# Where the stored weight sums of two down-projection products are kept, and the order of the last product's token tiles

## The chip, the cores and the metric

The kernel runs on one core of a Trainium2 chip. The metric is the device time of one execution in microseconds. It is written for five engines that run side by side: TensorE (PE, matmuls and transposes), VectorE (DVE), ScalarE (ACT), GpSimd (POOL) and SyncE (SP), which here issues most of the transfers between the memory of the chip and the on-chip buffers.

## The reference

Two layers over 512 tokens of width 1024, in fp32. Each layer mixes tokens and then applies a gated feed-forward part, and each half ends in a layer norm over the sum with its input:

```
for l in range(2):
    mix = token_mixing(x, ...)                      # projections, conv, two attentions, w_o
    x = layer_norm(ALPHA * x + mix, ...)
    h = causal_dwconv(x @ w_up, conv_w) + conv_b    # x: 512 x 1024, w_up: 1024 x 5632
    a, u = split(h)
    x = layer_norm(ALPHA * x + (gelu(a) * u) @ w_down, ...)   # w_down: 2816 x 1024
```

The change is in the last product, `(gelu(a) * u) @ w_down`, the down projection.

## The kernel before, in words

Every fp32 operand of a matmul is split into a high and a low part (`fp32r`), so that one product is three matmuls: high by high, high by low, low by high. For weights, SP loads a slice of up to 128 x 1024 numbers into a buffer `raw`, ACT rounds it into `wh`, and VectorE writes the remainder into `wl` (`unit` and `loaded`). `raw`, `wh` and `wl` rotate over three buffers each, so a slice can be loaded only when a slice three places earlier has been used.

The program is recorded first: every instruction goes to a list, with what it reads and writes (all instructions have line L445 for that reason). `schedule` (L322) then sets the order on each engine. It plays the program with modelled costs and takes, for an engine that is free, the instruction that stands first in the program among those whose inputs and buffers are there. A new place of an instruction in the program, or a new buffer for it, can therefore move others; once set, the order on each engine is fixed, SP's transfers included.

The down projection (`g_down`) saves products: both sides are cut into two by two blocks, and seven products of blocks and of sums of blocks replace eight. In the order of the program they are x1 (weight block 0), x2 (block 2), x6 (weight sum R), x5 (weight sum P), x7 (weight sum Q), x3 (block 3), x4 (weight sum Z); the text calls a product by its left operand or by its weight sum. Each of the seven has six weight slices `u` (the last of half size) and two token tiles of 128 tokens, `i` = 0 and 1, and is 66 matmuls of 128 x 512. `product` runs over the slices, and within a slice over both tiles (`part`); the last two slices are taken together, so that tile 0 is finished a little ahead of tile 1 and `done(0)` (additions to the residual and statistics on VectorE) can begin.

The four weight sums are worked out earlier in the layer and stored in the chip's memory. P and Q are stored whole (`sums`) and are split after loading. R and Z are stored already split (`parts`): `split_before` loads the high part straight into a `wh` buffer and the low part straight into a `wl` buffer, two transfers on SP's queue for a slice.

Three other kinds of buffers matter. `big()` gives one of eleven buffers of 128 x 2048 numbers, which hold the gated inputs of the down projection (`src.h`) and, two slices at a time, the split left operands that `halves` makes. `new_x()` gives the one pair `xh`, `xl` of 128 x 4096 numbers that holds the split input X of a layer's half; it is read for the last time by the last matmul of `w_up`, and taken again when the first tile of the next layer's input is normalized. Matmuls add up in banks: `a` (two of kind `sc`) serve x1, R, Q and Z.

A finished tile of the down projection is normalized by `g_norm`: statistics, a power of -0.5 on GpSimd, two steps on VectorE for each half of the row, a transfer to memory, and in layer 0 eight transposes and a split, which give the next layer's input. Tiles 0 and 1 are finished by x3, tiles 2 and 3 by Z. In the next layer `g_halves` runs its first three projections over tokens 0 to 255 (tiles 0 and 1) and then over tokens 256 to 511, which need tiles 2 and 3; the low parts of their weights are written on GpSimd.

Of the kernel before, what the change touches and what calls it, by code (L numbers as in the profile page):

```python
# [10 lines left out]
F32 = mybir.dt.float32  # L11
F32R = mybir.dt.float32r
# [491 lines left out]
def trunk(ctx, tc, xT_d, x_d, w_d, cst_d, sm_d, w1_d, gb_d, out_d, order):  # L504
# [3 lines left out]
    T, Y = Engine(rec, "PE", nc.tensor), Engine(rec, "SP", nc.sync)  # L508
# [5 lines left out]
    def pool(name, **kw):  # L514
        return ctx.enter_context(tc.tile_pool(name=name, **kw))

    cp = pool("cst", bufs=1)
    sb = pool("sb", bufs=1)
# [12 lines left out]
    cp, sb, smp, ps, dp = (RPool(p) for p in (cp, sb, smp, ps, dp))  # L531

    def nm(s):
        uid[0] += 1
        return f"{s}_{uid[0]}"

    def big(dt=F32):
        return sb.tile([128, 4, 512], dt, tag="big", bufs=11, name=nm("big"))
# [10 lines left out]
    def bank(tag):  # L549
        return ps.tile([128, 512], F32, tag=tag, bufs=dict(mm=3, sc=2, tp=2, pv=1)[tag], name=nm(tag))  # L550
# [14 lines left out]
    def mm3(o, ah, al, bh, bl, start, stop, **kw):  # L565
        mm(o, ah, bh, start, False, **kw)
        mm(o, ah, bl, False, False, **kw)
        mm(o, al, bh, False, stop, **kw)
# [13 lines left out]
    def loaded(src, n, lo=None):  # L582
        raw = sb.tile([128, 1024], F32, tag="raw", bufs=3, name=nm("raw"))
        wh = sb.tile([128, 1024], F32R, tag="wh", bufs=3, name=nm("wh"))
        wl = sb.tile([128, 1024], F32R, tag="wl", bufs=3, name=nm("wl"))
        Y.dma_start(raw[:, :n], src)
        A.activation(wh[:, :n], raw[:, :n], AF.Copy)
        (lo or V).tensor_tensor(wl[:, :n], raw[:, :n], wh[:, :n], op=sub)
        return wh, wl

    def split_before(hi, lo, n):
        wh = sb.tile([128, 1024], F32R, tag="wh", bufs=3, name=nm("wh"))
        wl = sb.tile([128, 1024], F32R, tag="wl", bufs=3, name=nm("wl"))
        Y.dma_start(wh[:, :n].bitcast(F32), hi)
        Y.dma_start(wl[:, :n].bitcast(F32), lo)
        return wh, wl

    def unit(*key, parts=1, lo=None):
        i = len(order)
        order.append(key)  # L600
        n = 1024
        if key[1] == "n_v":
            n = 280 * (key[2][1] - key[2][0])
        if key[1] == "w_dn" and key[3] == NFF // 4:
            n = 512
        raw = sb.tile([128, 1024], F32, tag="raw", bufs=3, name=nm("raw"))
        wh = sb.tile([128, 1024], F32R, tag="wh", bufs=3, name=nm("wh"))
        wl = sb.tile([128, 1024], F32R, tag="wl", bufs=3, name=nm("wl"))
        for p in range(parts):
            c = slice(p * n // parts, (p + 1) * n // parts)  # L610
            Y.dma_start(raw[:, c], w_d[i, :, c])
            A.activation(wh[:, c], raw[:, c], AF.Copy)
            (lo or V).tensor_tensor(wl[:, c], raw[:, c], wh[:, c], op=sub)
        return wh, wl
# [75 lines left out]
    def new_x():  # L690
        return (sb.tile([128, 8, 512], F32R, tag="xh", bufs=1, name=nm("xh")),
                sb.tile([128, 8, 512], F32R, tag="xl", bufs=1, name=nm("xl")))


    def g_down(l, src, r, st, nx, g_norm, last):
# [5 lines left out]
        NM = len(hv)  # L701
        nks = [2] * (NM - 1) + [1]
# [32 lines left out]
        def product(x, w, o, start, done):  # L735

            nu = NM
            kw = {} if start else dict(skip_group_check=True)
            for u in range(nu):
                n = 512 * nks[u]  # L740
                if isinstance(w, int):
                    ws = unit(l, "w_dn", w, u)
                elif w[0] < 2:
                    ws = loaded(src.sums[:, w[0], u * 1024:u * 1024 + n], n)
                else:
                    ws = split_before(*(src.parts[:, 2 * w[0] - 4 + j, u * 1024:u * 1024 + n] for j in range(2)), n)
                if u < nu - 2:
                    group = [(u, ws)]
                    for i in range(2):
                        part(x, group, o[i], i, start and u == 0, False, kw)  # L750
                    yield None
                elif u == nu - 2:
                    group = [(u, ws)]
                else:
                    group.append((u, ws))
                    for i in range(2):
                        part(x, group, o[i], i, False, True, kw)
                        done(i)
                        yield None

        def part(x, group, o, i, start, stop, kw):
            ks = [(u, k, ws) for u, ws in group for k in range(nks[u])]
            for a, (u, k, ws) in enumerate(ks):
                xh, xl = x[2 * u + k]
                c = slice(k * 512, k * 512 + 512)
                mm3(o, xh[:, TOK[i]], xl[:, TOK[i]], ws[0][:, c], ws[1][:, c], start and a == 0, stop and a == len(ks) - 1, **kw)
# [24 lines left out]
        P, Q, R, Z = ([i] for i in range(4))  # L791
        a, b = [bank("sc"), bank("sc")], [bank("pv"), bank("mm")]
        x1 = halves(A(0, 0))
        yield from product(x1, 0, a, True, first_of(0, 0, a, add))
        x2 = halves(A(0, 1))
        yield from product(x2, 2, b, True, then_stats(0, 0, more_of(0, 0, b, add)))
        x6 = halves(A(1, 0))
        yield from product(x6, R, a, False, first_of(0, 1, a, sub))
        c = [bank("mm"), bank("mm")]
        x5 = halves(sums(A(1, 0), A(0, 0)))  # L800
# [8 lines left out]
    def g_tok_norm(l, kind, nk, lhs, res_d, gi, last):  # L809
# [51 lines left out]
        if kind == "w_dn":  # L861
            yield from g_down(l, lhs, r, st, nx, g_norm, last)
            return nx[0], evs, res
# [574 lines left out]
```

## Time and profile before

| what | us |
| --- | --- |
| time, median of 3 runs | 1812.81 |
| lowest and highest of them | 1810.87 and 1815.93 |
| profiled execution | 1815.82 |
| its span | 1813.8 |
| TensorE busy | 1772.5 |
| VectorE, ScalarE, GpSimd busy | 1248.8, 824.9, 227.4 |

The profiled execution is one more execution, with a record of every instruction; its span goes from the first instruction to the last. In the rows below, a line gives when a group of instructions began, how long it was busy, its engine, what it wrote from what (names without their numbers), how many there were, and in square brackets how long the engine had stood still before and what it waited for. TensorE's matmuls overlap, so a single one shows a longer time than the distance to the next: 66 in 14.96 us are 0.227 us each.

### The profile page before, as it was taken

The numbers are of one execution on the slowest core, as the hardware profiler recorded it, in microseconds if no ns is written. First come the engines' busy times: TensorE is split into PE (matmuls) and PEld (weight loads), VectorE is DVE, ScalarE is ACT, GpSimd is POOL, SyncE is SP. The second block draws the span as 40 slices with busy tenths as digits, with TensorE's granted clock in tenths as the row PEclk, the third lists the DMA queues.
The fourth block names the chain that finished last, engine by engine and source line by source line (L and its number), as shares of the span: only waits on it lengthen the run. The fifth ranks groups of instructions, "written<-read, shape, count | busy, mean of one in ns | idle before, by whom it ended". The sixth has DMA issues, their size and how long they took to land.

```text
span 1813.8 us, 23525 instructions
## 1 busy us (share of the span) xinstructions
PE 1772.5 (98%) x8596; PEld 1482.3 (82%) x8596; DVE 1248.8 (69%) x2206; ACT 824.9 (45%) x1418; POOL 227.4 (13%) x302
## 2 busy tenths in 40 slices
PE   8999999999999999999999999999999999999996
PEld 7888888888888888887788887888888888888784
DVE  6978877534458788586679698774344678875884
ACT  4558855322324444354244587553223244444450
POOL 1300023000032110000123001220000411000002
PEclk9999999999999999999999999999999999999998
DMA  6520243233237886446644202332333377763654
GB/s 221 146 98 24 63 131 104 82 107 133 94 104 245 296 293 247 142 156 230 235 157 138 70 34 81 108 105 93 104 129 104 120 274 275 280 235 133 212 195 174
DMA packets 85683, 279.90 MB, mean 154 GB/s; under 512 B 10112, under 2 KB 12256, under 8 KB 85440
## 3 DMA queue, kind: packets, MB, share of 16 engines
q1 hardware_dynamic: 65536, 218.92, 35.4%
q0 software_dynamic: 20032, 59.48, 10.3%
q8 instruction: 68, 1.11, 0.2%
q14 instruction: 47, 0.39, 0.1%
HBM read 223.83 MB, written 42.99 MB: 147 GB/s over the span
## 4 chain that ended last, share of the span: by engine, by line
PE 90%; DVE 3%; DMA 2%; issue 2%; POOL 2%; ACT 1%; SPq 0%; DVEq 0%; POOLq 0%; ACTq 0%
PE mm L445 71%; PE sc L445 11%; PE pv L445 5%; PE tp L445 3%; DVE tmp L445 2%; DMA wh<-parts 1%; POOL wl L445 1%; POOL s L445 1%; DMA raw<-in_w_dram 0%; DMA wl<-parts 0%; DVE st L445 0%; DVE wl L445 0%; DVE s L445 0%; POOL tmp L445 0%; ACT L445 0%
## 5 line engine op out<-in xcount | busy, mean ns | idle before, releaser
L445 PE MATMUL mm<-xh,wh 128*128 128x512 f32 (+1 forms) x1632 | 621.4, 382 | 9.1 <-ACT wh L445 6.1
L445 PE MATMUL mm<-xh,wl 128*128 128x512 f32 (+1 forms) x1632 | 619.0, 380 | 0.6 <-POOL wl L445 0.6
L445 PE MATMUL mm<-xl,wh 128*128 128x512 f32 (+1 forms) x1632 | 619.4, 380 | 0.2 <-DVE xl L445 0.2
L445 ACT ACTIVATE wh<-raw 128x1024 fp32r<-128x1024 f32 (+2 forms) x307 | 317.8, 1038 | 534.5 <-PE mm L445 431.0
L445 DVE TENSOR_TENSOR wl<-raw,wh 128x1024 fp32r<-128x1024 f32 (+3 forms) x292 | 350.7, 1204 | 301.8 <-ACT wh L445 296.6
L445 PEld LDWEIGHTS mm<-xh,wh 128*128 128x128 f32 x1632 | 308.7, 189 | 62.3 <-ACT wh L445 6.5
L445 PEld LDWEIGHTS mm<-xh,wl 128*128 128x128 f32 x1632 | 309.1, 189 | 56.8 <-POOL wl L445 0.8
L445 PEld LDWEIGHTS mm<-xl,wh 128*128 128x128 f32 x1632 | 309.4, 190 | 53.5 <-DVE xl L445 0.8
L445 ACT ACTIVATE tmp<-tmp,s 128x512 f32<-128x512 f32 (+3 forms) x261 | 140.3, 558 | 72.3 <-DVE s L445 39.4
L445 PE MATMUL sc<-wh,big 128*128 128x512 f32 x416 | 136.1, 400 | 11.0 <-DMA wh<-parts 11.0
L445 DVE SCALAR_TENSOR_TENSOR tmp<-mm,smf,tmp 128x511 f32<-128x511 f32 (+1 forms) x176 | 131.1, 745 | 12.7 <-ACT tmp L445 10.5
L445 PE MATMUL mm<-wh,big 128*128 128x512 f32 x380 | 121.7, 390 | 0.0
L445 PE MATMUL mm<-big,wh 128*128 128x512 f32 x384 | 120.0, 391 | 0.0
L445 PEld LDWEIGHTS sc<-wh,big 128*128 128x128 f32 x416 | 80.1, 193 | 31.3 <-DMA wh<-parts 14.6
L445 DVE CUSTOM_DVE_ANT_0 tmp<-sc,cst 128x512 f32<-128x512 f32 (+3 forms) x192 | 89.8, 483 | 21.9 <-PE sc L445 20.5
L445 PE MATMUL tp<-cst,tmp 128*128 128x128 f32 x544 | 86.0, 274 | 5.6 <-DVE tmp L445 2.9
L445 POOL TENSOR_TENSOR tmp<-tmp,cst 128x512 f32<-128x512 f32 (+1 forms) x46 | 48.1, 1053 | 305.2 <-ACT pt L445 119.6
L445 DVE TENSOR_TENSOR big<-big,big 128x512 f32<-128x512 f32 (+3 forms) x114 | 85.8, 767 | 0.4 <-ACT big L445 0.2
L445 PEld LDWEIGHTS tp<-cst,tmp 128*128 128x128 f32 x544 | 67.2, 141 | 21.6 <-DVE xl L445 3.6
L445 ACT ACTIVATE tmp<-tmp 128x512 f32<-128x512 f32 (+2 forms) x68 | 41.1, 605 | 96.0 <-DVE tmp L445 95.8
L445 ACT ACTIVATE big<-big 128x512 fp32r<-128x512 f32 (+2 forms) x86 | 59.2, 713 | 53.9 <-DVE big L445 46.5
L445 PEld LDWEIGHTS mm<-big,wh 128*128 128x128 f32 x384 | 71.7, 188 | 14.4
(149 smaller groups left out, 2243.2 us busy)
## 6 DMA issues: line engine op xcount, KB each, us to landing
raw<-in_w_dram SPq DMA_DIRECT2D x269, 512.0 KB, 3.3
big<-in_w_dram SPq DMA_DIRECT2D x44, 512.0 KB, 5.5
parts<-big POOLq DMA_DIRECT2D x22, 1024.0 KB, 5.6
sums<-big POOLq DMA_DIRECT2D x22, 512.0 KB, 4.4
raw<-sums SPq DMA_DIRECT2D x20, 512.0 KB, 3.6
wl<-parts SPq DMA_DIRECT2D x20, 512.0 KB, 4.9
wh<-parts SPq DMA_DIRECT2D x20, 512.0 KB, 5.8
big<-big POOLq DMA_DIRECT2D x48, 128.0 KB, 2.7
```

Source lines behind the costliest of these rows:

```text
L445: op.call(*[f(x) for x in op.args], **{k: f(v) for k, v in op.kw.items()})
```

## The change

Two of the seven products get their stored sums in other buffers, and one of them another order of its tiles.

- R (x6): the first four slices go into the pair of `new_x()`, high parts into one and low parts into the other, by eight transfers. The last two slices still use `wh` and `wl`.
- Z (x4): all six slices are loaded whole, two slices in a pair of `big` buffers, twelve transfers into six buffers. Then all slices are run for token tile 0, `done(0)` follows, and all slices for tile 1.
- `split_before` is gone; `fetch` issues the two transfers of a slice and `stored` fills a pair of large buffers.

```diff
-    def split_before(hi, lo, n):
-        wh = sb.tile([128, 1024], F32R, tag="wh", bufs=3, name=nm("wh"))
-        wl = sb.tile([128, 1024], F32R, tag="wl", bufs=3, name=nm("wl"))
-        Y.dma_start(wh[:, :n].bitcast(F32), hi)
-        Y.dma_start(wl[:, :n].bitcast(F32), lo)
-        return wh, wl
...
+            if w == Z:
+
+                ws = [stored(w, m, big(F32R), big(F32R)) for m in range((NM + 1) // 2)]
+                for i in range(2):
+                    for u in range(nu):
+                        part(x, [(u, [f[:, u % 2 * 1024:] for f in ws[u // 2]])], o[i], i, False, u == nu - 1, kw)
+                        if u < nu - 1:
+                            yield None
+                    done(i)
+                    yield None
+                return
+            if w == R:
+                early = new_x()
             for u in range(nu):
...
+                elif u < 4:
+                    ws = [f[:, 2 * u:2 * u + 2].rearrange("p a c -> p (a c)") for f in early]
+                    fetch(w, u, ws, n)
                 else:
-                    ws = split_before(*(src.parts[:, 2 * w[0] - 4 + j, u * 1024:u * 1024 + n] for j in range(2)), n)
+                    ws = [sb.tile([128, 1024], F32R, tag=tag, bufs=3, name=nm(tag)) for tag in ("wh", "wl")]
+                    fetch(w, u, ws, n)
...
+        def fetch(w, u, to, n):
+            for j in range(2):
+                Y.dma_start(to[j][:, :n].bitcast(F32), src.parts[:, 2 * w[0] - 4 + j, u * 1024:u * 1024 + n])
+
+        def stored(w, m, *to):
+            to = [f.rearrange("p a c -> p (a c)") for f in to]
+            for u in range(2 * m, min(2 * m + 2, NM)):
+                c = u % 2 * 1024
+                fetch(w, u, [f[:, c:c + 1024] for f in to], 512 * nks[u])
+            return to
```

The order moves at these places. SP's queue in layer 0, at the end of `w_up` and during x1, before (`raw` from `in_w_dram` are slices of weight blocks: `raw_6838` is x1's fifth, `raw_6870` its last, of half size, `raw_6898` x2's first):

```order
L445 DMA raw_6762<-in_w_dram 128x1024
L445 DMA raw_6838<-in_w_dram 128x1024
L445 DMA raw_6870<-in_w_dram 128x512
L445 DMA raw_6898<-in_w_dram 128x1024
L445 DMA raw_6918<-in_w_dram 128x1024
L445 DMA raw_6939<-in_w_dram 128x1024
L445 DMA raw_6974<-in_w_dram 128x1024
```

R's first transfer stands nine places behind x2's first slice there. And after (`raw_6842` is x1's fifth slice, `raw_6880` its last, `raw_6910` x2's first; `xh_6847` and `xl_6834` are the pair of `new_x()`, `parts_5309` the stored sums):

```order
L445 DMA raw_6762<-in_w_dram 128x1024
L445 DMA xl_6834<-parts_5309 128x1024
L445 DMA raw_6842<-in_w_dram 128x1024
L445 DMA xh_6847<-parts_5309 128x1024 x2
L445 DMA xl_6834<-parts_5309 128x1024
L445 DMA xh_6847<-parts_5309 128x1024
L445 DMA xl_6834<-parts_5309 128x1024
L445 DMA raw_6880<-in_w_dram 128x512
L445 DMA xh_6847<-parts_5309 128x1024
L445 DMA xl_6834<-parts_5309 128x1024
L445 DMA raw_6910<-in_w_dram 128x1024
L445 DMA raw_6936<-in_w_dram 128x1024
```

Six of R's eight transfers stand ahead of x1's last slice now, and all eight ahead of x2's first.

TensorE in layer 0 at x1's last slice, before (`sc_6851` is a bank of x1, `pv_6982` and `mm_6995` those of x2):

```order
L445 MATMUL sc_6851<-wh_6891,big_6799 128x512
L445 MATMUL sc_6851<-wh_6921,big_6799 128x512
L445 MATMUL sc_6851<-wl_6931,big_6799 128x512
L445 MATMUL sc_6851<-wh_6921,big_6799 128x512
L445 MATMUL pv_6982<-wh_6956,big_6815 128x512
L445 MATMUL pv_6982<-wl_6965,big_6815 128x512
L445 MATMUL pv_6982<-wh_6956,big_6815 128x512 x2
L445 MATMUL pv_6982<-wl_6965,big_6815 128x512
L445 MATMUL pv_6982<-wh_6956,big_6815 128x512
L445 MATMUL mm_6995<-wh_6956,big_6815 128x512
```

Here x2 follows x1. And after (`sc_6838` and `sc_6855` are x1's banks, and R's too):

```order
L445 MATMUL sc_6838<-wl_6979,big_6799 128x512
L445 MATMUL sc_6838<-wh_6977,big_6799 128x512
L445 MATMUL sc_6855<-wl_6979,big_6799 128x512
L445 MATMUL sc_6855<-wh_6977,big_6799 128x512
L445 MATMUL sc_6838<-xh_6847,big_6955 128x512
L445 MATMUL sc_6838<-xl_6834,big_6955 128x512
L445 MATMUL sc_6838<-xh_6847,big_6955 128x512 x2
L445 MATMUL sc_6838<-xl_6834,big_6955 128x512
L445 MATMUL sc_6838<-xh_6847,big_6955 128x512
L445 MATMUL sc_6855<-xh_6847,big_6955 128x512
```

R's matmuls follow x1's at once; x2's come between later ones of R.

SP's queue in layer 0 ahead of Z, before (`raw_7524` is x3's last slice, `raw_7537`, `raw_7565` and `raw_7570` the next layer's first, `res` the residual that the norm stores):

```order
L445 DMA raw_7524<-in_w_dram 128x512
L445 DMA raw_7537<-in_w_dram 128x1024
L445 DMA raw_7565<-in_w_dram 128x1024
L445 DMA raw_7570<-in_w_dram 128x1024
L445 DMA wl_7575<-parts_5309 128x1024
L445 DMA wh_7580<-parts_5309 128x1024
L445 DMA wl_7596<-parts_5309 128x1024
L445 DMA wh_7603<-parts_5309 128x1024
L445 DMA wh_7612<-parts_5309 128x1024
L445 DMA wl_7614<-parts_5309 128x1024
L445 DMA res_7619<-tmp_6847 128x512
L445 DMA res_7619<-tmp_6859 128x512
```

The next layer's first slices stand ahead of Z's there, and Z's transfers go on, slice by slice, for eight more places between the stores. And after (`big_7525` to `big_7571` are Z's six buffers, `raw_7581` and on the next layer's first slices):

```order
L445 DMA raw_7518<-in_w_dram 128x512
L445 DMA big_7525<-parts_5309 128x1024 x2
L445 DMA big_7533<-parts_5309 128x1024 x2
L445 DMA big_7544<-parts_5309 128x1024
L445 DMA big_7549<-parts_5309 128x1024
L445 DMA big_7544<-parts_5309 128x1024
L445 DMA big_7549<-parts_5309 128x1024
L445 DMA big_7564<-parts_5309 128x1024
L445 DMA big_7571<-parts_5309 128x1024
L445 DMA big_7564<-parts_5309 128x512
L445 DMA big_7571<-parts_5309 128x512
L445 DMA raw_7581<-in_w_dram 128x1024
```

All of Z's transfers stand in a block behind x3's last slice now, and the next layer's first three slices behind them.

## Rows read from the trace of the kernel before

**Rows 1.** The page's busy times of the engines (share of the span, instructions).

```profile
PE 1772.5 (98%) x8596; PEld 1482.3 (82%) x8596; DVE 1248.8 (69%) x2206; ACT 824.9 (45%) x1418; POOL 227.4 (13%) x302
```

**Rows 2.** TensorE's waits: line, what it waited for, us in total, times, longest.

```profile
PE sc L445 <- DMA wh<-parts: 11.0, 9, 2.6
```

**Rows 3.** The chain of waits, layer 0, x1 to R: start, duration (us), work.

```profile
786.26 14.96 PE sc L445 x66
...
812.28 6.42 DMA wh<-parts
...
834.95 5.21 PE mm L445 x23
```

**Rows 4.** The chain of waits, layer 1, x1 to R.

```profile
1684.53 14.96 PE sc L445 x66
...
1713.94 5.85 DMA wh<-parts
...
1732.36 14.96 PE mm L445 x66
```

**Rows 5.** TensorE's timeline, layer 1, Z: start, duration, operation, count, idle before.

```profile
1776.85 0.39 PE L445 MATMUL mm<-wh,big 128*128 128x512 f32 x1
...
1794.10 1.22 PE L445 MATMUL sc<-wh,big 128*128 128x512 f32 x2 [2.44 <-DMA wh<-parts]
...
1801.34 0.39 PE L445 MATMUL sc<-wh,big 128*128 128x512 f32 x1
```

**Rows 6.** Windows: length, busy per engine, clock share (PEclk), transfer share, GB/s.

```profile
884.00:888.00 4.00, 4.00 (x15) 3.19 (x14) 3.83 (x8) 0.25 (x1) 0.78 (x2) 0.77 0.95 310
...
916.00:920.00 4.00, 3.92 (x19) 3.49 (x18) 1.30 (x2) 0.76 (x2) 0.00 (x0) 0.57 0.02 4
...
1796.00:1800.00 4.00, 4.00 (x11) 3.17 (x10) 0.00 (x0) 0.00 (x0) 0.00 (x0) 0.50 0.01 5
818.00:822.00 4.00, 3.26 (x14) 2.71 (x15) 2.09 (x4) 0.00 (x0) 0.00 (x0) 1.00 1.03 414
```

**Rows 7.** TensorE's timeline, layer 0, Z and the passage to layer 1.

```profile
879.44 0.39 PE L445 MATMUL mm<-wh,big 128*128 128x512 f32 x1
881.84 1.78 PE L445 MATMUL tp<-cst,tmp 128*128 128x128 f32 x8 [2.01 <-DVE tmp L445]
...
902.64 0.39 PE L445 MATMUL sc<-wh,big 128*128 128x512 f32 x1
...
914.87 1.26 PE L445 MATMUL tp<-cst,tmp 128*128 128x128 f32 x8 [1.65 <-DVE xl L445]
916.21 0.73 PE L445 MATMUL mm<-xh,wh 128*128 128x256 f32 x3
```

**Rows 8.** The page's transfer issues: count, KB each, us to landing.

```profile
raw<-in_w_dram SPq DMA_DIRECT2D x269, 512.0 KB, 3.3
```

**Rows 9.** VectorE's timeline, layer 0, end of x1.

```profile
795.25 0.68 DVE L445 TENSOR_TENSOR wl<-raw,wh 128x512 fp32r<-128x512 f32 x1
```

**Rows 10.** VectorE's timeline, x4's splits in layers 0 and 1.

```profile
870.11 2.23 DVE L445 TENSOR_TENSOR big<-big,big 128x512 fp32r<-128x512 f32 x4
...
1767.53 2.22 DVE L445 TENSOR_TENSOR big<-big,big 128x512 fp32r<-128x512 f32 x4
```

**Rows 11.** VectorE's timeline, layer 0, normalization of tiles 2 and 3.

```profile
904.79 2.36 DVE L445 SCALAR_TENSOR_TENSOR tmp<-tmp,s,pt 128x512 f32<-128x512 f32 x2
909.96 1.41 DVE L445 SCALAR_TENSOR_TENSOR tmp<-tmp,s,pt 128x512 f32<-128x512 f32 x2 [2.81 <-POOL s L445]
```

**Rows 12.** GpSimd's timeline beside it.

```profile
903.53 2.41 POOL L445 TENSOR_TENSOR wl<-raw,wh 128x1024 fp32r<-128x1024 f32 x1 [2.68 <-ACT wh L445]
```

**Rows 13.** VectorE's timeline, end of the program.

```profile
1801.07 1.38 DVE L445 SCALAR_TENSOR_TENSOR tmp<-tmp,sc 128x512 f32<-128x512 f32 x2 [18.29 <-PE sc L445]
...
1803.99 5.74 DVE L445 SCALAR_TENSOR_TENSOR tmp<-tmp,s,pt 128x512 f32<-128x512 f32 x7
```

**Rows 14.** SP's queue, end of the program.

```profile
1806.76 3.83 SPq L445 DMA_DIRECT2D out_dram<-tmp  x4
```

## The prediction

> **What bounds the kernel now.** I read the page's busy times first: TensorE is busy for 1772.5 us, 98% of the span [rows 1]. So only what TensorE loses can be won, 1813.8 - 1772.5 = 41.3 us of waiting and what a lowered clock adds to the busy time, and each loss has to be found by its place. The list of TensorE's waits came next: the largest item is matmuls into `sc` banks waiting for a transfer of stored weight sums (`wh<-parts`), 11.0 us in 9 waits [rows 2]. The two products that use them are R, the third of the seven products of the down projection, and Z, the last. Then I followed the chain of waits through R. In layer 0 the stretch of x1, x2 and R starts at 786.26 and the next product starts at 834.95 [rows 3]. Each product is 66 matmuls and takes 14.96 us without a gap (the x66 pieces), so three should end at 786.26 + 44.88 = 831.14: R loses 3.8 us. In layer 1 it is 1684.53 + 44.88 = 1729.41 against 1732.36 [rows 4], 2.95 us. In both the chain names the load of `wh` just before the loss: R's slices share three rotating buffers with x2's, so their loads are issued late, and one behind another takes 5.85 to 6.42 us.
>
> For Z I read the timeline of TensorE. In layer 1 x3's last matmul starts at 1776.85 and, at 0.227 us each (14.96 / 66), ends at 1777.08; Z's last starts at 1801.34, so Z takes 24.5 us where 14.96 are needed: 9.5 us lost [rows 5]. The largest wait is 2.44 us, and its price is more than itself: after it the granted clock is 0.50 in the window 1796 to 1800, the lower of the two levels (1.2 and 2.4 GHz) [rows 6]. In layer 0 Z's stretch holds the passage into the next layer too: x3 ends at 879.67, the first transpose waits 2.01 us for DVE (881.84), and after the halves of the next layer's first projections the transposes wait 1.65 us again, so that the second halves start at 916.21 [rows 7], at a clock of 0.57 up to 920 [rows 6], which costs 0.43 x 4 = 1.7 us: as if they had started at 917.9.
>
> **R's loads.** The change issues eight loads of 512 KB as soon as the last `w_up` matmul has read X, at about 786.3 in layer 0, between x1's own weights. A load of 512 KB alone takes 3.3 us [rows 8]; in a full window the queue moves 414 GB/s [rows 6], 1.27 us for each, so 2.03 us of the 3.3 are fixed. Eight loads, x1's fifth and last slices (512 and 256 KB) between them: R's last lands at about 786.3 + 2.0 + 9.5 x 1.27 = 800.4, before x1 ends at 801.22. R's matmuls then run without waits, which gives back 3.8 and 2.95 us.
> What it costs: x1's last slice comes behind six of these loads and lands at about 797.9 instead of some 3 us before its rounding; DVE wrote its low part at 795.25 so far, for 0.68 us [rows 9]. Behind its rounding on ACT (about as long) and DVE's other work of those microseconds it is ready at about 800.9, where TensorE wants it at 801.22 - 6 x 0.227 = 799.9 to 800.2: 0.9 us. R also accumulates into the banks that x1 has just filled, and DVE must read them first: 0.55 us (DVE's 0.68 us less what the other bank covers). Its bounds: 0, if DVE keeps its old order, and 4 us, if x2's first slice, which now also comes behind the burst, is waited for as well. I take 1.45 us a layer, nearer to the first end because x2's matmuls are not wanted until R's have begun. R's part: 3.8 + 2.95 - 2 x 1.45 = 3.85 us.
>
> By the Trainium skill ("DMA: Bandwidth & Descriptors", section "Where 436 GB/s comes from") transfers from HBM to SBUF are held to about 358 GB/s a core, so an estimate is 1.46 us for each load, and R's last would land at 802.2, after x1's end. The window above shows 414 GB/s over four microseconds, and so I keep 1.27; the sum by the rule would be up to 9.5 x 0.19 = 1.8 us a layer less.
>
> **Z's loads.** Twelve loads (ten of 512, two of 256 KB) go into six large buffers that hold until then the split gated inputs (released by x4's splits on DVE, the last of which end at 872.3 and 1769.8 [rows 10]) and x3's first input, released by TensorE two slices into x3, about 870. They start at about 869.2 and 1766.5 and land from 872.5 to 885.3, and from 1770 to 1782.6, 11 x 1.27 + 2 us. TensorE starts Z at 879.7 and 1777.1 and in the new order (tile 0 through all slices, then tile 1) wants slice 2 at 3.2 us (2 x 6 matmuls, and the transposes) and slice 4 at 7.8 us after the start; they land 4.0 and 3.5 us ahead of that. So no wait is left in Z of layer 1: 9.5 us. Its bounds: 0, if the loads wait for the buffers until x3 ends, and 10.3, the clock's share in the last slice included. The cover is a margin of 3.5 us; I take 9.5.
>
> **The tile order.** With tile 0 done half a product (7.5 us) before tile 1, only one tile's normalization stands behind the last matmul. At the end of the program DVE runs seven normalizing steps in 5.74 us, 0.82 each, and two additions and two stats steps [rows 13]; the output's last four transfers start at 1806.76 [rows 14]. From Z's end at 1801.57 to the span's end, 1813.8, are 12.2 us. Three steps (2.46), an addition (0.69) and a stats step (about as long) fewer are 3.8; about 0.8 of it comes back because the one tile must wait for its own power step on GpSimd, which two tiles hid behind each other. I take 3.0, of bounds 1.5 and 3.8.
>
> In the passage between the layers, TensorE must do Z (14.96), 32 transposes (0.16 each at most, by the eight at 914.87) and 72 matmuls of half the columns (0.114 each, 8.2 us) after 879.67: it reaches the second halves at 907.8 if nothing waits. They need tile 3's normalization. In the trace Z's last matmul ends at 902.9 and the second halves start at 916.21 [rows 7], 13.3 us for the normalizations of tiles 2 and 3. With tile 2 done during Z, an addition and a stats step (1.4), four normalizing steps (2.8) and the splits of one tile (about 0.6) go from behind Z, and 8.5 us are left. Z itself now ends at about 897 (14.96 and the transposes of two tiles). That is 905.5, before TensorE wants it. But GpSimd's three splits of the next layer's weights fall into these normalizations: beside one of them (903.53, 2.41 us [rows 12]) two DVE steps took 2.36 us instead of 1.41 [rows 11], and the power step of a normalization queues behind them on GpSimd. One such step late by one or two splits is 907.9 to 910.3, with DVE's own 0.95 us up to 911.3; so the second halves start at about 910 at full clock, against 917.9: I take 8.0, of bounds 4 (a third split ahead of it, and the clock lowered once more) and 10.1, nothing late.
>
> The Trainium skill ("SBUF — State Buffer", section "Who interferes with whom") says why: DVE and GpSimd share a pair of ports, and a DVE instruction with two SBUF inputs blocks against a GpSimd one that reads SBUF. The trace agrees with 0.95 us for two steps. Without this loss the passage would give about 9.
>
> **The sum.** 3.85 + 9.5 + 3.0 + 8.0 = 24.4 us. The profiled execution took 1815.82 us (span 1813.8), so 1791.4 on that; it is 3.0 us above the median of 1812.81, on which it gives 1788.4. I forecast 1789 us.
>
> **The rivals.** *R's burst delays x1 and x2.* If the loads move at the 310 GB/s of the window 884 to 888, whose transfer engines were 95% busy [rows 6], instead of 414, each takes 1.69 us, x1's last slice comes at about 801, x2's first at 806, and three or four microseconds are lost a layer, as much as R wins. For it: TensorE has nothing else to do there, and loads behind others took up to 6.42 us [rows 3]. Against: in the full window of R itself the queue held 414 GB/s. Then R's part is -1 to -4 instead of +3.85: 1793 to 1796.
> *Z's loads come late.* If the first large buffer is released only at x3's end, the first slice lands 2.0 + 2 x 1.27 = 4.6 us after that, and in layer 0 the next layer's first weights stand behind all twelve loads on the in-order queue. Z gains 4 instead of 9.5, the passage 2 instead of 8: 3.85 + 4 + 3 + 2 = 12.9 us in all, 1800, and up to 1804 if those weights are waited for too. Against it stand x4's splits ending 7.4 us before x3 does [rows 10].
> *Slower.* R's eight loads stand before x1's last and x2's first slices on SP's queue, and no later load can pass them. x2's first slice is behind 10.5 loads' worth of transfers now. TensorE wants it about 15.7 us after the first has begun to move (x1's 14.96 us and the part of R whose input is ready), and runs dry when they take longer: a load in the burst that takes t costs 10.5 t - 15.7 a layer, nothing at 1.27. It decides from t of 2.6 us, where two layers lose 23 us and eat all other gains: above 1813. The rows give half that time.
> *Nothing happens*, because the buffers are held by something not seen here and the order falls back: 1809 to 1816.
>
> **How the numbers follow.** Forecast 0.63 (its own range 1783 to 1793), R's burst 0.20, Z late 0.10, no effect 0.04, slower 0.03. A change of 0.3%, 5.4 us, is about what a measurement of this kernel can tell from none. Faster by more than that are the first three, 0.93; the same 0.04; slower 0.03. The range of 1782 to 1799 leaves out the late Z and the last two, 0.17, and a little of the forecast's lower side.
>
> **What would show it.** Right: no wait on `parts` in TensorE's list; three products from 786 to about 833; Z of layer 1 in about 15 us with the clock at 1.0; one tile behind the last matmul, about 9 us; the second halves from about 910. Wrong: waits of matmuls in x1's last slice or x2's first for ACT or DVE (R's burst); the first matmul of Z waiting for a load; the second halves not earlier than 915.

## The result, and the profile after

The changed kernel takes 1792.81 us (median of 4 runs, 1791.56 to 1794.97), the kernel before 1812.9 beside it: a ratio of 0.9889, 95% interval 0.9872 to 0.9906. That is 20.1 us faster; 1789 was forecast, with a range of 1782 to 1799. The profiled execution took 1793.08 us with a span of 1791.3, 22.5 us less than the span of before, against 24.4 forecast.

Both programs run the same 8596 matmuls and transposes, so I matched them by their number in the two traces and read by how much a matmul starts earlier. The gain of a part is the difference between two such points; the last part runs from Z's last matmul to the span's end. All profiled kernels below are measured so, against the first profile of before.

| kernel (profile) | R, layer 0 | passage | R, layer 1 | Z, layer 1 | end | span |
| --- | --- | --- | --- | --- | --- | --- |
| forecast | 2.35 | 8.0 | 1.5 | 9.5 | 3.0 | |
| the changed kernel | 2.30 | 5.3 | 1.47 | 9.52 | 3.9 | 1791.3 |
| R alone, first and second profile | 2.4, 2.5 | 3.5, 2.1 | 1.4, 1.2 | 2.1, 4.2 | 0.4, 0.3 | 1803.0, 1802.7 |
| Z alone, first and second profile | -1.3, -0.8 | 5.1, 4.3 | -2.2, -0.1 | 9.5, 9.5 | 3.9, 3.9 | 1798.1, 1795.9 |
| Z's old tile order, both layers | 2.4 | 10.6 | 1.3 | 9.5 | 2.6 | 1787.1 |
| low parts on VectorE, all places | 2.2 | 6.6 | 1.0 | 9.5 | 3.9 | 1793.5 |
| low parts on VectorE, passage | 2.1 | 10.6 | 1.5 | 9.5 | 3.9 | 1785.8 |
| old order in layer 0 only | 2.2 | 10.2 | 1.4 | 9.5 | 3.9 | 1785.2 |
| old order, GpSimd kept busy | 2.4 | 5.2 | 1.0 | 9.5 | 2.6 | 1791.9 |
| R's loads on GpSimd's queue | 2.3 | 6.6 | 0.6 | 9.5 | 3.9 | 1791.9 |
| two early slices of R | 1.6 | 10.1 | 1.1 | 9.5 | 3.9 | 1787.5 |
| before, second profile | -1.2 | -1.5 | -2.8 | 3.8 | 0.0 | 1814.9 |

"R" runs from the first matmul of x1 to that of the product after R, "passage" from there to x1 of layer 1. Ahead of x1 of layer 0 the profiles differ from that of before by up to 1.3 us either way, which no part contains (and by another 4.4 us where all low parts are on VectorE).

The list of TensorE's waits of the changed kernel (columns as in [rows 2]) no longer has `parts` in it. Transposes wait 4.2 us for `tmp`, where they waited 2.9 us before, and 1.1 us for `xl`, where they waited 2.7:

```profile
PE tp L445 <- DVE tmp L445: 4.2, 4, 1.9
...
PE tp L445 <- DVE xl L445: 1.1, 2, 0.5
PE sc L445 <- DVE tmp L445: 0.8, 3, 0.3
PE sc L445 <- ACT wh L445: 0.6, 2, 0.3
```

The chain of the changed kernel at x1's end and through R, which answers to [rows 3]:

```profile
789.50 9.87 DMA raw<-in_w_dram
...
799.45 0.64 ACT wh L445
...
800.14 1.47 PE sc L445 x4
...
801.63 0.70 DVE tmp L445
...
802.37 5.28 PE sc L445 x22
...
824.88 7.77 PE sc L445 x34
832.65 7.48 PE mm L445 x33
```

x1's last slice is in flight for 9.87 us, TensorE waits for it and then for VectorE, which reads the banks; the product after R starts at 832.65 instead of 834.95. In its full windows the burst held about the rate that was assumed, 387 to 416 GB/s (length of the window, busy time of each engine, clock, transfer share, GB/s):

```profile
790.00:794.00 4.00, 4.00 (x19) 3.33 (x18) 3.67 (x6) 1.97 (x4) 0.55 (x1) 1.00 1.02 416
794.00:798.00 4.00, 4.00 (x19) 3.31 (x18) 3.82 (x8) 0.82 (x2) 0.00 (x0) 1.00 1.03 399
798.00:802.00 4.00, 3.72 (x15) 2.18 (x13) 3.14 (x6) 0.96 (x2) 0.00 (x0) 1.00 1.02 387
```

Z of layer 1, one line of TensorE's timeline in place of [rows 5]: 66 matmuls without a gap.

```profile
1768.05 15.12 PE L445 MATMUL sc<-big,big 128*128 128x512 f32 x66
```

It ends at 1783.0, and 8.3 us later the span is over. What did not come as forecast is the passage. TensorE's timeline of the changed kernel, against [rows 7]:

```profile
887.07 7.31 PE L445 MATMUL sc<-big,big 128*128 128x512 f32 x31
...
897.67 0.63 PE L445 MATMUL tp<-cst,tmp 128*128 128x128 f32 x4 [1.51 <-DVE tmp L445]
900.43 1.09 PE L445 MATMUL tp<-cst,tmp 128*128 128x128 f32 x4 [1.89 <-DVE tmp L445]
...
910.10 0.62 PE L445 MATMUL mm<-xh,wh 128*128 128x256 f32 x3
```

Z ends at 894.2 and not at 897, as I had reckoned; 2.3 us of that is R's gain, which the reckoning left out. For the same reason the second halves' start at 910.10 is not the 910 of the forecast: 2.3 us of it are R's, and the passage itself has brought 3.8 us up to there (the other 1.4 us of its 5.3 come behind it, where the clock of before was 0.57 [rows 6]). TensorE stands twice in the middle of the first halves, at tile 2's transposes, and runs at a clock of 0.57 behind that:

```profile
896.00:900.00 4.00, 1.03 (x8) 0.69 (x6) 4.00 (x2) 0.60 (x1) 3.73 (x2) 1.00 0.18 71
900.00:904.00 4.00, 3.57 (x18) 3.60 (x19) 3.90 (x9) 0.60 (x1) 0.84 (x2) 0.57 0.69 216
```

In the first of these windows VectorE is busy for all 4 us with two instructions. Its timeline, with tile 2's four normalizing steps first together and then one by one, and GpSimd's show why:

```profile
889.20 0.69 DVE L445 SCALAR_TENSOR_TENSOR tmp<-tmp,sc 128x512 f32<-128x512 f32 x1 [0.53 <-PE sc L445]
...
891.08 9.20 DVE L445 SCALAR_TENSOR_TENSOR tmp<-tmp,s,pt 128x512 f32<-128x512 f32 x4
```

```profile
891.08 2.99 DVE L445 SCALAR_TENSOR_TENSOR tmp<-tmp,s,pt 128x512 f32<-128x512 f32 x1
...
894.00 0.74 DVE L445 SCALAR_TENSOR_TENSOR tmp<-tmp,s,pt 128x512 f32<-128x512 f32 x1
...
894.66 2.86 DVE L445 SCALAR_TENSOR_TENSOR tmp<-tmp,s,pt 128x512 f32<-128x512 f32 x1
...
897.45 2.83 DVE L445 SCALAR_TENSOR_TENSOR tmp<-tmp,s,pt 128x512 f32<-128x512 f32 x1
```

```profile
890.95 0.22 POOL L445 TENSOR_SCALAR s<-s 128x1 f32<-128x1 f32 x1 [7.37 <-DVE s L445]
891.13 2.40 POOL L445 TENSOR_TENSOR wl<-raw,wh 128x1024 fp32r<-128x1024 f32 x1
893.49 1.02 POOL L445 TENSOR_TENSOR s<-s,mhalf 128x1 f32<-128x1 f32 x1
894.48 5.26 POOL L445 TENSOR_TENSOR wl<-raw,wh 128x1024 fp32r<-128x1024 f32 x2
```

Tile 2's four normalizing steps took 9.20 us; tile 0's, with GpSimd idle but for its power step, took 2.74 (at 877.41). Three of the four were stretched, and each of them ends 0.54 to 0.55 us after one of GpSimd's three splits (which end at 893.53, 896.98 and 899.74); the second step ran beside the power step, between two splits, and kept its 0.74 us. The splits themselves lost little: 7.66 us for the three.

That they start just there comes from the fixed order on GpSimd too. ACT had rounded the first slice at 888.89 and all three at 890.78, but tile 2's scalar step stands ahead of the splits on GpSimd, which stood still for it until 890.95. The new tile order with the splits ahead of that step was not run.

### The profile page after: what moved, and what is told of

Its sections match the earlier page's. It is cut to its first block, busy times and chain, and to the rows that moved or that the text cites. A ratio compares the mean times of both kernels' runs of the same rounds, so it can differ in the third digit from the quotient of the medians.

```text
span 1791.3 us, 23495 instructions
## 1 busy us (share of the span) xinstructions
PE 1765.7 (99%) x8596; PEld 1480.6 (83%) x8596; DVE 1255.5 (70%) x2206; ACT 824.7 (46%) x1418; POOL 228.2 (13%) x302
## 4 chain that ended last, share of the span: by engine, by line
PE 92%; DVE 3%; DMA 1%; issue 1%; POOL 1%; ACT 1%; SPq 0%; DVEq 0%; ACTq 0%; POOLq 0%
PE mm L445 73%; PE sc L445 10%; PE pv L445 6%; PE tp L445 3%; DVE tmp L445 2%; DMA raw<-in_w_dram 1%; POOL wl L445 1%; DVE wl L445 0%; POOL s L445 0%; ACT wh L445 0%; DVE st L445 0%; DVE s L445 0%; ACT L445 0%; SPq L445 0%; DVE xl L445 0%
## 5 line engine op out<-in xcount | busy, mean ns | idle before, releaser
L445 PE MATMUL sc<-big,big 128*128 128x512 f32 (+2 forms) x388 | 93.5, 355 | 0.0
L445 PE MATMUL sc<-wh,big 128*128 128x512 f32 x264 | 83.9, 391 | 0.6 <-ACT wh L445 0.6
```

The source lines that it names most:

```text
L445: op.call(*[f(x) for x in op.args], **{k: f(v) for k, v in op.kw.items()})
```

## The experiments

**R alone, Z alone.** The two parts apart. R alone leaves Z's block and its order out:

```diff
-            if w == Z:
...
-                ws = [stored(w, m, big(F32R), big(F32R)) for m in range((NM + 1) // 2)]
...
-                return
...
-                elif u < 4:
+                elif w == R and u < 4:
```

> R's slices go into the pair of new_x() as in the changed kernel; Z keeps its alternating tiles and its loads into wh and wl. By matching matmuls one by one, the changed kernel gains 2.30 us in layer 0's R and 1.47 us in layer 1's R. Theory (the parts are independent): this kernel gains those 3.8 us and nothing else, a median of about 1809. Rival (R's early loads also take transfers out of Z's way, or Z's gain needs them): 5 us or more, or the start of the product after R in layer 0 not at 832.5.

Z alone leaves the early loads out:

```diff
-            if w == R:
-                early = new_x()
...
-                elif u < 4:
-                    ws = [f[:, 2 * u:2 * u + 2].rearrange("p a c -> p (a c)") for f in early]
-                    fetch(w, u, ws, n)
```

> Z is loaded whole and runs tile 0 and then tile 1; R is loaded as before. Theory: passage 5.2 + layer 1's Z 9.5 + end 3.9 = 18.7 us of the changed kernel's 22.5, a median of 1795 to 1797; the product after R starts at 834.95 as before. Rival (the parts overlap): less than 16 us.

R alone took 1806.66 us (ratio 0.9963, 0.9949 to 0.9978), 6.6 us less than before where 3.8 were expected. R itself gave 2.4 and 1.4 us as it should; the rest came in the passage and in Z, whose instructions this kernel does not change. Z alone took 1801.29 us (0.9932, 0.9918 to 0.9946), later than the 1795 to 1797 expected: passage, Z and end gave 18.5 us, but R lost 1.3 and 2.2. Both misses sat at places that had no edit, so I profiled these two kernels and the one before a second time.

**The second profiles.** Three kernels unchanged.

> The kernel before, unchanged, for a second profile. In its first profile the clock fell in the passage (0.80, 0.77 and 0.57 in the windows 880 to 888 and 916 to 920), in the run with R alone it did not at the same waits. Theory (whether the clock falls at a wait of 2 us differs from one execution to the next): the same waits within 0.1 us, and at some of them another clock. Rival (the clock follows from the order of the kernel): the same clock in the same windows, within 0.05.

> R alone in the new buffers, a second profile. In the first the passage was 3.55 us and layer 1's Z 2.1 us shorter than in the kernel before, at the same waits but a higher clock. Theory (chance of the execution): some of it is gone here, the gain of R itself stays 2.2 to 2.5 us in layer 0 and 1.3 to 1.6 us in layer 1. Rival (it belongs to the kernel): passage and Z again 3 to 4 and 2 us shorter.

> Z alone in the new buffers and order, a second profile. In the first R lost 1.3 us more in layer 0 and 2.2 us more in layer 1 than in the kernel before, behind the same wait of 2.9 us, at a clock of 0.68. Theory (chance of the execution): the clock behind these waits differs here from the first profile in one layer at least. Rival (it belongs to the kernel): 0.68 again in both. Passage about 5 us, layer 1's Z 9.5 us, end 3.9 us again under both.

In the second profile of before (1816.91 us) three windows read, of R in layer 0, R in layer 1 and Z in layer 1:

```profile
820.00:824.00 4.00, 4.00 (x14) 3.16 (x14) 0.00 (x0) 0.00 (x0) 0.00 (x0) 0.73 0.65 264
...
1720.00:1724.00 4.00, 3.86 (x11) 3.07 (x12) 0.50 (x1) 0.00 (x0) 0.00 (x0) 0.59 0.88 341
...
1796.00:1800.00 4.00, 2.45 (x10) 1.40 (x9) 0.00 (x0) 0.00 (x0) 0.00 (x0) 1.00 0.72 270
```

In the first profile the same windows read:

```profile
820.00:824.00 4.00, 4.00 (x19) 3.32 (x18) 0.09 (x1) 0.00 (x0) 0.00 (x0) 1.00 0.94 323
...
1720.00:1724.00 4.00, 4.00 (x18) 3.31 (x19) 0.46 (x1) 0.94 (x2) 0.00 (x0) 1.00 1.01 346
```

and 0.50 for Z [rows 6]. So the same program lost 5.75 us at R of layer 1 instead of 2.95, and 5.7 at Z of layer 1 instead of 9.5. Z alone shows it too: behind R's wait the clock was 0.68 in its first profile and 1.00 in its second:

```profile
820.00:824.00 4.00, 4.00 (x14) 3.10 (x13) 0.00 (x0) 0.00 (x0) 0.00 (x0) 0.68 0.70 232
```

```profile
820.00:824.00 4.00, 3.85 (x17) 2.90 (x16) 0.00 (x0) 0.42 (x1) 0.00 (x0) 1.00 0.97 344
```

By themselves these windows do not show a clock that falls behind one and the same wait in one execution and not in the next, because the waits differ as well. From x2's last matmul to R's first it is 2.94 us in the first profile of before and 3.47 in the second in layer 0, and 2.14 and 3.93 in layer 1; with Z alone it is 2.93 and 2.58, and 2.75 and 2.56. In each of these four pairs the clock fell in the execution with the longer wait, and so it did in Z of layer 1 of before (longest wait of TensorE 2.44 us in the first profile, 1.43 in the second). But Z of layer 1 with R alone goes the other way: the longest wait is 1.75 us in the first profile and 2.78 in the second, and the clock behind it is the lower one in the first:

```profile
1785.00:1789.00 4.00, 3.48 (x9) 2.46 (x9) 0.00 (x0) 0.00 (x0) 0.00 (x0) 0.57 0.23 90
```

```profile
1783.00:1787.00 4.00, 3.50 (x15) 2.58 (x15) 0.00 (x0) 0.00 (x0) 0.00 (x0) 1.00 0.88 336
```

So at R and Z my theory holds in part: the waits for transfers and the clock behind them both change from one execution of a program to the next, and the length of the wait does not decide.

In the passage, of which my expectation spoke, it failed. The clock of the second profile of before fell again behind the same two waits (windows of 880 to 888 and 916 to 924):

```profile
884.00:888.00 4.00, 4.00 (x12) 3.10 (x12) 3.96 (x9) 0.60 (x1) 0.78 (x2) 0.62 0.96 304
916.00:920.00 4.00, 3.58 (x18) 3.14 (x19) 2.16 (x4) 1.19 (x2) 0.00 (x0) 0.72 0.33 123
```

With R alone it stayed at 1.00 there in both profiles, behind waits of the same length (2.40 and 2.0 us between two matmuls). The lowered clock cost 0.20, 0.23 and 0.43 of three windows of 4 us, 3.4 us in all, in the first profile of before; so most of what R alone gains in the passage goes with the kernel and not with the execution. Why R's early loads should change a clock some 50 us and more later stays open. In Z of layer 1, R alone gained 2.1 and 4.2 us, which two profiles do not settle.

**Z's old tile order, whole loads.** Only the order of the tiles is taken back:

```diff
             if w == Z:
-                ws = [stored(w, m, big(F32R), big(F32R)) for m in range((NM + 1) // 2)]
-                for i in range(2):
...
-                return
+                zs = [stored(w, m, big(F32R), big(F32R)) for m in range((NM + 1) // 2)]
...
+                elif w == Z:
+                    ws = [f[:, u % 2 * 1024:] for f in zs[u // 2]]
```

> As the changed kernel, but Z alternates its tiles slice by slice and takes the last two slices together, as before; the loads into the large buffers stay. Theory: Z of layer 1 still takes 15 us (the loads alone give the 9.5 us), the end after Z's last matmul goes back from 8.3 to about 12.2 us, and the passage loses more, since both tiles' normalization stands behind Z beside GpSimd's splits: 1799 to 1803. Rival (the order is worth nothing, the loads do all): 1793, the end at 8.3 us.

1789.08 us (0.9864, 0.9851 to 0.9878): faster than the changed kernel, where I expected 6 to 10 us slower. Z of layer 1 kept its 9.5 us and the passage gained 10.6 us instead of 5.3. The end went back only from 3.9 to 2.6, where I expected all of it to go: most of the end's gain comes with the loads. Before, VectorE's two additions stand together at Z's end (1801.07 [rows 13], where Z ends at 1801.57); here the first comes 1.8 us ahead of Z's end at 1777.4:

```profile
1775.59 0.69 DVE L445 SCALAR_TENSOR_TENSOR tmp<-tmp,sc 128x512 f32<-128x512 f32 x1 [7.42 <-PE sc L445]
```

My theory on the passage fell: I thought that the splits would meet both tiles here. GpSimd's timeline and VectorE's of this kernel:

```profile
888.82 7.13 POOL L445 TENSOR_TENSOR wl<-raw,wh 128x1024 fp32r<-128x1024 f32 x3 [5.64 <-ACT wh L445]
```

```profile
891.98 0.69 DVE L445 SCALAR_TENSOR_TENSOR tmp<-tmp,sc 128x512 f32<-128x512 f32 x1 [3.47 <-PE sc L445]
...
895.79 1.41 DVE L445 SCALAR_TENSOR_TENSOR tmp<-tmp,s,pt 128x512 f32<-128x512 f32 x2
897.65 4.06 DVE L445 SCALAR_TENSOR_TENSOR tmp<-tmp,s,pt 128x512 f32<-128x512 f32 x6 [0.46 <-POOL s L445]
```

The splits start at 888.82, 2.3 us earlier than in the changed kernel, because here they stand ahead of the tiles' scalar steps on GpSimd, and both tiles come later. So the splits are over at 895.95 and the eight steps take about 0.7 us each. The addition at 891.98, whose second input is a bank, keeps its 0.69 us beside a split.

**Low parts on VectorE.** The other way to part the two engines: the new order stays, the splits leave GpSimd (`lo=G` in `unit` puts them there).

```diff
-                    w = first.pop(0) if first else unit(*key, lo=G)
+                    w = first.pop(0) if first else unit(*key)
```

> As the changed kernel, but the low parts of the next layer's first weights are written by VectorE instead of GpSimd. Theory (GpSimd's three splits block VectorE's normalizing steps of tile 2, which took 9.20 us for four instead of 2.74): the four take 2.7 to 2.9 us plus at most three splits of 1.2 us between them, TensorE's waits of 1.51 and 1.89 us for tile 2's transposes and the clock of 0.57 behind them go, the passage gains 2 to 4 us more: 1789 to 1791. Rival (the transposes' place among the first halves is the cause, or VectorE loses as much to its three more splits): 1792 to 1794, with a wait at the transposes.

1798.05 us (0.9918, 0.9904 to 0.9931): slower than the changed kernel, so the expectation failed. But the passage up to the next layer's own work gained 10.7 us; the loss is at the two other places that use this function, ahead of `w_up` in each layer, some 4.4 us each. There the transposes wait for `xl` from VectorE, about 3 us each time:

```profile
PE tp L445 <- DVE xl L445: 6.1, 2, 3.0
```

In layer 0 this wait ends at 545.00. Just ahead of the `xl` it is for, VectorE has four normalizing steps, where in the changed kernel that `xl` comes first (at 543.32). The first low part of a weight follows only at 545.58; so this wait comes from another order on VectorE, and not from the splits' own time:

```profile
541.62 2.73 DVE L445 SCALAR_TENSOR_TENSOR tmp<-tmp,s,pt 128x512 f32<-128x512 f32 x4
544.26 1.28 DVE L445 TENSOR_TENSOR xl<-tp,xh 128x512 fp32r<-128x512 f32 x2
```

So I did it in the passage alone (`n_kv` are the weights of the layer that begins there):

```diff
-                    w = first.pop(0) if first else unit(*key, lo=G)
+                    w = first.pop(0) if first else unit(*key, lo=None if key[1] == "n_kv" else G)
```

> As the changed kernel (tile 0 ahead of tile 1), but VectorE writes the low parts of the three slices between the layers alone; at the other two places per program, where the run before lost 4.4 us each, GpSimd does again. Theory (GpSimd's splits block tile 2's normalizing steps, 9.20 us instead of 2.74): the passage gains 10 to 11 us as in that run instead of 5.2, nothing is lost elsewhere: 5.3 us below the changed kernel, 1786 to 1789. Rival (the loss at the other places belongs to the same shift of work and comes up later): 1790 or more.

1788.61 us (0.9859, 0.9835 to 0.9883), passage 10.6 us, as the theory has it. Tile 2's four steps on VectorE, behind one split of its own:

```profile
890.72 1.23 DVE L445 TENSOR_TENSOR wl<-raw,wh 128x1024 fp32r<-128x1024 f32 x1
891.87 2.73 DVE L445 SCALAR_TENSOR_TENSOR tmp<-tmp,s,pt 128x512 f32<-128x512 f32 x4
```

The transposes also stand at other places on TensorE in this kernel, so alone it does not tell the two causes apart. The next run tests GpSimd's work with TensorE's order almost unchanged.

**GpSimd kept busy.** The suspected cost is put where it was absent: into the kernel with the old order, whose sequence on TensorE it leaves almost as it was (14 of 8596 places differ). `rec.bias = 300` ranks the new instructions 300 places later in the order from which `schedule` takes.

```diff
...
             rs = rsqrt(mv[:, 1:2], 1, r1, o1)
+            if not last and kind == "w_dn" and t in (2, 3):
+                rec.bias = 300
+                d = tmp()
+                G.tensor_scalar(d, mask, mv[:, 0:1], None, op0=add)
+                for _ in range(2):
+                    G.tensor_tensor(d, d, mask, op=add)
             rec.bias = 0
```

> The kernel with Z's old order in both layers, with two additions and one scalar addition of 128x512 on GpSimd put behind the statistics of tile 2 and of tile 3 in layer 0; their results are used by nothing. Theory (GpSimd's work blocks VectorE's two-input steps): the normalizing steps, which took 1.41 us for two and 4.06 us for six there, take 2 to 5 us longer in all, tile 3's transposes and the second halves come 2 to 4 us later: 1791 to 1793 instead of 1789. Rival (only the transposes' place on TensorE counted): the steps keep 0.68 us each, the time stays 1789.

1793.4 us (0.9887, 0.9863 to 0.9912), 4.3 us above the same kernel without it; the passage fell from 10.6 to 5.2 us. Tile 3's last two steps took 3.44 us, where two took 1.41, beside GpSimd's additions, and its transposes came late; first VectorE, then GpSimd, then TensorE:

```profile
901.16 3.44 DVE L445 SCALAR_TENSOR_TENSOR tmp<-tmp,s,pt 128x512 f32<-128x512 f32 x2 [0.46 <-POOL s L445]
```

```profile
901.10 5.85 POOL L445 TENSOR_TENSOR tmp<-tmp,cst 128x512 f32<-128x512 f32 x4
```

```profile
905.25 1.97 PE L445 MATMUL tp<-cst,tmp 128*128 128x128 f32 x8 [2.75 <-DVE xl L445]
```

Part of the loss is the power step queued behind the added work, and part a clock of 0.59 and 0.56 from 904 to 912.

**Old order in layer 0 only.** Each layer gets the order that suits what stands behind it (the whole loads stay in both, as `zs`):

```diff
...
+                ws = zs
+            if w == Z and last:
                 for i in range(2):
...
+                elif w == Z:
+                    ws = [f[:, u % 2 * 1024:] for f in zs[u // 2]]
```

> As the changed kernel, but Z alternates its tiles in layer 0 (as in the run with the old order) and runs tile 0 ahead of tile 1 in the last layer alone. Theory (the new tile order costs about 5 us in the passage and gives about 1.3 us at the end): span 5 us below the changed kernel's and 1.3 us below the old order's in both layers: 1786 to 1789. Rival (the old order's gain is another thing than the passage): 1792 as the changed kernel.

1787.96 us (0.9856, 0.9827 to 0.9886): the passage 10.2 us and the end 3.9. It is 25 us below the kernel before and 5 us below the changed one, the best of these kernels; the old order in both layers and the low parts on VectorE in the passage lie within about 1 us of it, which these runs do not order.

**R's remaining 1.5 us.** Two tries. R's loads on GpSimd's queue:

```diff
-                    fetch(w, u, ws, n)
+                    fetch(w, u, ws, n, G)
...
```

> As the changed kernel, but R's eight early loads are issued on GpSimd's queue instead of SP's. In the changed kernel R's part loses 1.5 us a layer: TensorE waits 0.67 us and some for x1's last slice and 0.7 us for VectorE to read the banks. Theory (x1's last slice is late because it stands behind six loads on SP's queue): it comes early again, the wait at x1's last slice goes, the product after R starts 0.7 to 0.9 us earlier in each layer; the time 1791 to 1792. Rival (it is late because the loads share the transfer engines' rate, whatever their queue): the same wait, the time 1793, or later, as GpSimd's loads start later.

1794.76 us (0.9893, 0.9869 to 0.9918). The wait at x1's last slice went, but in x2, which stands ahead of R again there, distances of 0.9 and 0.75 us between two matmuls took its place, for low parts that VectorE writes (R's loads, among transfers of the residual on the same queue, were up to 16 us in flight). R gained 2.3 and 0.6 us, no better. And only two slices early, on top of the kernel with the old order in layer 0:

```diff
-                elif u < 4:
+                elif u < 2:
```

> As the kernel with Z's old order in layer 0 and the new one in the last layer (1787.96), but only the first two of R's slices go into the pair of new_x(), by four early transfers; the other four use wh and wl. Theory (x1's last slice is late because of the six loads ahead of it, 0.8 us of the 1.5 us that R still loses): the wait at x1's last slice goes, but R's later slices wait for the rotating buffers again, 1 to 3 us a layer: 1788 to 1793. Rival (four early transfers are enough): 0.8 us a layer better, 1786.

1790.3 us (0.9871, 0.9852 to 0.9891), 2.3 us slower; in the profiles, 0.9 us of that is in R, and 1.4 us stands ahead of x1 of layer 0, where nothing was edited. R's later slices waited again, as expected, but the wait at x1's last slice did not go: 0.81 us between two matmuls, although the slice landed at 796.8 instead of 799.4. The chain of this run goes through VectorE, which has the splits for R's operand and the sums for a later one ahead of that slice:

```profile
797.90 0.56 DVE big L445
...
799.11 1.02 DVE tmp L445 x2
800.13 0.61 DVE wl L445
...
800.79 0.74 PE sc L445 x2
```

So the six loads ahead of the slice do not decide alone: without four of them the slice lands early, and VectorE's sequence holds its low part to 800.1 all the same.

## Why the prediction was right, and where its sum was off

- **R.** 2.30 and 1.47 us against 2.35 and 1.5. The loss of 1.45 us a layer was right in size, and so were its two halves, the last slice and the banks. For the first half I named both the loads and VectorE's other work; in the changed kernel the slice's landing comes last, and the run with two early slices shows VectorE holding it as long without that. The rival of the burst did not happen: 387 to 416 GB/s in the full windows. That the agreement is this close is luck in part, for what R lost before is a draw: measured against the second profile of before, R gains 3.5 and 4.3 us.
- **Z's loads.** No wait, 9.52 us against 9.5 in layer 1 (5.7 against the second profile of before).
- **The end.** 3.9 us instead of 3.0: 8.3 us stand behind Z's last matmul, not 9.2. But I put it down to the tile order, and the loads with the old order keep 2.6 us of it, which leaves the new order some 1.3 us, less than the 1.5 of my lower bound. That the size came out near is luck. The new order without the whole loads was not run.
- **The passage.** The term that was mis-sized: "two DVE steps took 2.36 us instead of 1.41", from which I took 0.95 us and a power step late by one or two splits. The mechanism was the right one, but I priced one meeting of the engines; in the changed kernel all three splits, rounded together by ACT from 887.84 to 890.78 and held on GpSimd behind tile 2's scalar step, met three of the four steps of tile 2. That cost 9.20 - 2.74 = 6.5 us on VectorE and two waits and a spell of lower clock on TensorE, 5.3 us of gain instead of 8.0. I also expected it at tile 3's end, and it came at tile 2's transposes, which stand ahead of most of the first halves.
- **From the profile to the median.** The parts sum to 22.5 us of span, the medians differ by 20.1. The profiled execution of before was 3.0 us above its median, that of the changed kernel 0.3. I took the whole 24.4 us from the median, although the losses that I was removing had been read in an execution above the median; the second profile shows that single losses differ by up to 3.8 us from one execution to another.

What nothing in the prediction weighed is that the new tile order might cost more than it gives. By the runs it gives 1.3 us at the end and costs about 5 in the passage; the gain of the change comes from the loads. With the loads and the old order, passage and end give 13.2 us. I had put 11.0 us down to the order for these two, and the changed kernel gave 9.2, so that this half of the sum came near by another way than the one I gave.

## What to carry to other kernels

When work is made ready earlier, look at what else becomes ready at the same moment: three weight splits on GpSimd that had been spread by waits now ran in one block, and moving a tile's normalization forward put it into that block, which GpSimd's fixed order then started right behind that tile's scalar step. Price such a meeting by all the instructions of both engines that can fall into it, not by the one pair that the old trace happens to show. And a loss read from a single profile is one draw: what R and Z lost to waits for transfers, with the clock behind them, differed by 0.5 to 3.8 us between two profiles of one program, so the sum is to be made against the median with a part of the loss only. The clock's loss in the passage stood in both profiles of before; a second profile helps to tell the two kinds apart.

## What was not expected of the hardware

VectorE's steps with two inputs in the on-chip buffers stretched from 0.74 us to 2.83 to 2.99 us beside GpSimd's two-input splits, while three splits took 7.66 us instead of 7.13; an addition with one input in a bank kept 0.69 us. By the Trainium skill ("SBUF — State Buffer", section "Who interferes with whom") a VectorE instruction with two inputs in SBUF contends with a GpSimd one that reads it, the lock is exclusive, and the order of issue decides who blocks. The trace agrees in that each of the three stretched steps ends 0.54 to 0.55 us after a split; the order it shows for only two of them, since the first began 0.05 us ahead of its split by the records (891.08 and 891.13) and was held all the same. With R alone the granted clock fell to 0.57 behind a wait of 1.75 us in one execution and stayed at 1.00 behind 2.78 us at the same product in another.
